# Modulation vectors of a two-block transformer: which MLP step computes which vector, and where VectorE's products and their sums over partitions are queued

## The chip, the cores and the metric

The kernel runs on one core of a Trainium2 chip. The metric is the device time of the whole program in microseconds (us). Five engines run side by side, each through its own queue of instructions in order: TensorE (PE; its weight loads are listed apart, as PEld), VectorE (DVE), ScalarE (ACT), GpSimd (POOL) and SyncE (SP), which issues the loads from memory. They wait for each other by semaphores.

## The reference, cut to what matters

A first block (a norm, two mixers, a mixture of experts) is followed by a second block of two layers, of which each is modulated by six vectors that come from one condition vector:

```python
cond = jax.nn.silu(c)                      # (1, 1024)
for i in range(2):
    mod = cond @ w_ada[i] + b_ada[i]       # 1024 x 6144
    sh1, sc1, g1, sh2, sc2, g2 = jnp.split(mod, 6, axis=-1)
    h = rms_norm_2(x, ln_mix_g[i]) * (1.0 + sc1[:, None, :]) + sh1[:, None, :]
    y = nsa_mixer(h, ...) if i == 0 else diff_mixer(h, ...)
    x = x + g1[:, None, :] * y
    h = rms_norm_2(x, ln_mlp_g[i]) * (1.0 + sc2[:, None, :]) + sh2[:, None, :]
    x = x + g2[:, None, :] * (jnp.square(jax.nn.relu(h @ w_mlp_in[i])) @ w_mlp_out[i])
```

There are 256 tokens of 1024 features, and the MLP is 4096 wide. The twelve vectors are numbered here as in the kernel, `mods[0]` to `mods[11]`, six to a layer: 5 is g2 of the first layer, 6 to 11 belong to the second. A vector is the condition times a weight of 1024 x 1024 in single precision, 4 MB.

## The kernel before

**Order of the work.** The kernel is written as one Python program, and a list scheduler (`schedule_with_timeline_sim=True`, line 2362) puts every engine's instructions into one fixed order, taking for each the place where its own simulation finds its operands ready. An instruction under `tc.issue_after(x)` is placed no earlier than x. Once placed, an engine goes through its queue in that order; where an instruction waits, all behind it wait.

**A vector on TensorE.** `ada_half` does half a vector: it loads two tiles of `w_ada` (1 MB each, tile `w`), and 32 matmuls add the condition's products into a bank `adaps`, four column strips side by side (in the order's listing 32 of the name `adaps<-w,cond`). VectorE copies or adds the bank to `ada_acc`. `ada_close` then sums over the four strips with two matmuls against `pick` (each shown as two in the trace; tile `adasum` of the pool `mm`), and VectorE adds the bias (`mod<-adasum,cols`).

**A vector on VectorE.** `ada_vector`, called four times for a vector, loads one tile of `w_ada` and adds two products of 128 x 1024 to the accumulator `adasum` in SBUF, one `TENSOR_SCALAR` for a vector's first and `SCALAR_TENSOR_TENSOR` for the other seven. With the fourth call, four matmuls against ones sum the accumulator over its partitions into `adaps` (`strips`, line 187; in the order's listing four of `adaps<-adasum,ones`), and ScalarE copies that to `ada_acc`; `ada_close` follows at the next call. There is one accumulator, so the next vector's first product waits for the strips of the one ahead.

**Where they are.** The first five halves come ahead of the first layer's attention. In it (`work(j)`, called for its 16 pairs) seven more are done, for j = 3 to 9, so that vector 5 is whole at its end. In the first layer's MLP (MLP 0), `mlp(0, ..., 11)` does vectors up to 10 on VectorE; vector 11 follows on TensorE after it, ahead of the second layer's attention. The second layer's MLP (MLP 1) does none.

**An MLP step.** The MLP goes in 8 steps of 512 hidden features, and the steps overlap: first the block `hp` (the product with `w_mlp_in`, line 448: 96 matmuls of 128 x 258 into four banks of `mm`), then the block `mlp` (the product of the step before with `w_mlp_out`, line 491: 96 matmuls of 128 x 256 into four banks of the pool `acc`). Each block takes two loaded tiles `w`, and each tile is split by halves into a high and a low part: ScalarE casts (`whi`, line 151), VectorE subtracts (`wlo`, line 152). There are three buffers of each, so that a cast waits until TensorE has used the pair three back. Behind an `hp` block VectorE and ScalarE form `hid` (`hb`, `relu`, squares). Three calls of `ada_vector` belong to a step, two after `hid`, one between the two tiles of `mlp`.

**Loads.** All 1 MB weight tiles come through one ring of 8 buffers by SyncE's queue. The tiles `adaps`, `adasum` and `hp` take turns in the four banks of `mm`.

Of the kernel before, what the change touches and what calls it, by code (L numbers as in the profile page):

```python
# [13 lines left out]
F32 = mybir.dt.float32  # L14
# [7 lines left out]
ALU = mybir.AluOpType  # L22
# [3 lines left out]
P = 128  # L26
T = 256
TX = T + 2
D = 1024
# [15 lines left out]
def block_kernel(ctx: ExitStack, tc: tile.TileContext, A: dict, out: bass.AP):  # L45

    nc = tc.nc
# [8 lines left out]
    def mm(shape=(P, 512), name="mm"):  # L56
        return mm_pool.tile(list(shape), F32, tag="mm", name=name)
# [117 lines left out]
    ada_at = [0, 0, 0.0]  # L175
# [42 lines left out]
    def ada_close():  # L218

        if not ada_open:  # L220
            return
        v = ada_open.pop()
        sp = mm(name="adasum")
        for c in range(2):
            nc.tensor.matmul(
                sp[:, 4 * c : 4 * c + 4], ada_acc[:, c * P : (c + 1) * P], pick, start=True, stop=True
            )
        nc.vector.tensor_tensor(
            mods[v].rearrange("p (j c) -> p c j", c=2),
            sp[:, 0:8].rearrange("p (c j) -> p c j", c=2),  # L230
            col("ada", v * KD, KD).rearrange("p (j c) -> p c j", c=2),
            op=ALU.add,
        )
# [8 lines left out]
            ada_at[2] -= 2.0  # L242
            ada_half()

    def ada_vector(acc):

        ada_close()
        v, q, _ = ada_at
        lay, i = divmod(v, 6)
        w = load(  # L250
            A["w_ada_2"][lay, 2 * q * P : 2 * (q + 1) * P, i * D : (i + 1) * D].rearrange("(k p) c -> p k c", p=P), D
        )
        for kk in range(2):
            c = cond[:, 2 * q + kk : 2 * q + kk + 1]
            if q + kk == 0:
                nc.vector.tensor_scalar(acc, w[:, kk, :], c, None, op0=ALU.mult)
            else:
                nc.vector.scalar_tensor_tensor(acc, w[:, kk, :], c, acc, op0=ALU.mult, op1=ALU.add)
        ada_at[1] = q + 1
        if q == 3:  # L260
            ps = mm(name="adaps")[:, :T]
            strips(ps, ones[:, 0:32], acc, True, True)
            nc.scalar.copy(ada_acc, ps)
            ada_at[:2] = [v + 1, 0]
            ada_open.append(v)

    def ada_until(v):
        while ada_at[0] < v:
            ada_half()
        if v - 1 in ada_open:  # L270
            ada_close()
# [168 lines left out]
    def proj_X_steps(w, c0, outs):  # L440

        for k0, t in colblock(w, c0, 512):
            for k1, hi, lo in halves(t):
                for kk in range(hi.shape[1]):
                    k = k0 + k1 + kk
                    for h in range(4):
                        for i, (a, b) in enumerate(passes((hi, lo), hX)):
                            nc.tensor.matmul(  # L448
                                outs[h],
                                a[:, kk, h * P : (h + 1) * P],  # L450
                                b[:, k, :],
                                start=(k == 0 and i == 0),
                                stop=(k == KD - 1 and i == 2),
                            )
                    yield
# [26 lines left out]
    def rows(w, r0, outs, acts, a0, first, after=None):  # L482


        t = load(w[r0 * P : (r0 + 2) * P, :].rearrange("(k p) c -> p k c", p=P), D)
        ada_credit(rate[0])
        parts = halves(t)

        def product(kk, hi, lo, dc):
            for i, (a, b) in enumerate(passes((hi, lo), acts)):  # L490
                nc.tensor.matmul(  # L491
                    outs[dc // 2][:, dc % 2, :],
                    a[:, 0, dc * P : (dc + 1) * P],
                    b[:, a0 + kk, :],
                    start=(first and kk == 0 and i == 0 and dc % 2 == 0),
                    stop=(after is not None and kk == 1 and i == 2 and dc % 2 == 1),
                )

        if after is None:
            for kk, hi, lo in parts:  # L500
                for dc in range(KD):
                    product(kk, hi, lo, dc)
            return
        with tc.manual_schedule(engines={mybir.EngineType.PE}):
            for pr in range(KD // 2):
                for kk, hi, lo in parts:
                    for dc in (2 * pr, 2 * pr + 1):
                        product(kk, hi, lo, dc)
                after(pr)
# [16 lines left out]
    def closing(banks, gate=None, st=None, each=None, feed=None):  # L526

        def after(pr):  # L530
            v = add_pair(pr, banks[pr], gate)
            last = pr == KD // 2 - 1
            if feed is not None:
                feed(pr)
                st.square(pr, v)
                if pr >= 2:
                    st.count(pr - 2)
                return
            if st is not None:
                if last and st.w is not None:  # L540
                    held["first"]["dve"] = added[0]
                st.square(pr, v)
            if st is not None:
                for p in range(pr - 2, pr + 1 if last else pr - 1):
                    if last and p == pr and st.w is None:
                        st.fill()
                    if p >= 0:
                        st.count(p)
            if each is not None:
                for p in range(pr - 1, pr + 1 if last else pr):  # L550
                    if p >= 0:
                        each(p)

        return after
# [1094 lines left out]
    def ct(name, shape, dt=F32, tag=None, **kw):  # L1649
        return pc.tile(list(shape), dt, name=name, tag=tag or name, **kw)  # L1650
# [87 lines left out]

    def mlp(lay, close, st, vectors):

        ada_sum = ct("adasum", (P, D), tag="klo")
        if ada_at[1]:
            ada_half()
        w_i, w_o = A["w_mlp_in_2"][lay], A["w_mlp_out_2"][lay]
        pend = None
        for j in range(9):
            rate[0] = 0.0
            if j < 8:
                hp = [(mm if j else acc)((P, TX), name="hp") for _ in range(4)]
                for n, _ in enumerate(proj_X_steps(w_i, j * 512, hp)):  # L1750
                    if j == 0 and n == 3:
                        st.count(2)
                        st.count(3)
                        rb = st.scale()
                both = n8("hid", F32R).rearrange("p (a k t) -> p a k t", a=2, k=4)
                for i in range(2):
                    r = sc((P, 2, T), name="relu")
                    b = pw.tile([P, 4], F32, tag="nm", name="hb")
                    for c in range(2):
                        nc.vector.tensor_copy(b[:, c : c + 1], hp[2 * i + c][:, T : T + 1])  # L1760
                        nc.vector.tensor_tensor(r[:, c, :], hp[2 * i + c][:, 0:T], rb, op=ALU.mult)
                        nc.scalar.activation(r[:, c, :], r[:, c, :], AF.Relu, bias=b[:, c : c + 1])
                    hi = both[:, 0, 2 * i : 2 * i + 2, :]
                    nc.scalar.activation(hi, r, AF.Square)
                    nc.scalar.activation(r, r, AF.Square)
                    nc.vector.tensor_tensor(both[:, 1, 2 * i : 2 * i + 2, :], r, hi.bitcast(F32), op=ALU.subtract)
                for _ in range(2):
                    if j and ada_at[0] < vectors:
                        ada_vector(ada_sum)
            if j == 0:  # L1770
                banks = [acc((P, 2, T), name="mlp") for _ in range(4)]
            if pend is not None:
                jj, bb = pend
                if jj == 7:
                    ada_close()
                    ada_until(6 * lay + 6)
                for c in (0, 2):
                    if c == 2 and ada_at[0] < vectors:
                        ada_vector(ada_sum)
                    after = close(banks) if jj == 7 and c == 2 else None  # L1780
                    rows(w_o, jj * 4 + c, banks, (bb[:, 0], bb[:, 1]), c, jj == 0 and c == 0, after)
            pend = (j, both)
# [395 lines left out]
    def work(j):  # L2178
        chains.tick(3)
        if 1 <= j < 5:  # L2180
            steps(second, 3)
        elif j >= 10:
            steps(first, 1)
        if 3 <= j < 10:
            ada_half()

    attention([(i, m) for i in range(8) for m in (1, 0)], pair_probs, pair_out, pair_tail, work)
# [16 lines left out]
    nc.vector.tensor_tensor(nlam, ls[:, 1:2], ls[:, 0:1], op=ALU.subtract)  # L2204
    nc.vector.tensor_scalar(nlam, nlam, -lam_init, None, op0=ALU.add)
    st = Stats()
    mlp(0, lambda banks: closing(banks, mods[5], st), st_x, 11)


    modulated(st, 1, 0, col("lnx", 8, 8))  # L2210
# [155 lines left out]
```

## Time and profile before

| | before |
|---|---|
| median of 3 runs | 1307.55 us |
| lowest and highest | 1306.39 and 1308.12 us |
| the profiled execution's own time | 1305.86 us |
| span of its trace | 1304.2 us |
| TensorE clock granted, mean | 0.99 of full |

The trace is of one execution. Its span leaves out 1.7 us around the program; its own time lies 1.7 us under the median of the runs. The stages that the change touches lie in the span's last 600 us: the first layer's attention from about 600 to 790 us, MLP 0 from 790 to about 985, the second layer's attention to 1113, MLP 1 to the end.

### The profile page before, as it was taken

The numbers are of one execution on the slowest core, as the hardware profiler recorded it, in microseconds if no ns is written. First come the engines' busy times: TensorE is split into PE (matmuls) and PEld (weight loads), VectorE is DVE, ScalarE is ACT, GpSimd is POOL, SyncE is SP. The second block draws the span as 40 slices with busy tenths as digits, with TensorE's granted clock in tenths as the row PEclk, the third lists the DMA queues.
The fourth block names the chain that finished last, engine by engine and source line by source line (L and its number), as shares of the span: only waits on it lengthen the run. The fifth ranks groups of instructions, "written<-read, shape, count | busy, mean of one in ns | idle before, by whom it ended". The sixth has DMA issues, their size and how long they took to land.

```text
span 1304.2 us, 22821 instructions
## 1 busy us (share of the span) xinstructions
PE 1260.6 (97%) x9471; PEld 998.6 (77%) x9471; DVE 651.8 (50%) x1268; ACT 511.8 (39%) x918; POOL 65.2 (5%) x92
## 2 busy tenths in 40 slices
PE   8999899999999999999998999999999999999998
PEld 7779565665555556556885679999997879999998
DVE  6765310130101111004776777698667787655554
ACT  7743211111101111113455656544544564654644
POOL 1010000000000000000410000000001120000000
PEclk9999899999999999998998999999999999999999
DMA  7997799999999999998554845599677532555510
GB/s 252 363 411 300 289 421 420 421 421 421 421 420 420 421 421 421 420 415 305 167 195 153 328 164 199 182 353 338 249 272 271 178 130 77 180 172 187 194 66 33
DMA packets 99157, 373.98 MB, mean 287 GB/s; under 512 B 10649, under 2 KB 14442, under 8 KB 74730
## 3 DMA queue, kind: packets, MB, share of 16 engines
q1 hardware_dynamic: 99050, 372.49, 75.1%
q8 instruction: 76, 1.25, 0.4%
q14 instruction: 31, 0.25, 0.1%
HBM read 371.41 MB, written 1.05 MB: 286 GB/s over the span
## 4 chain that ended last, share of the span: by engine, by line
PE 74%; issue 11%; DVE 2%; ACT 1%; POOL 0%; DVEq 0%; ACTq 0%; POOLq 0%
PE hp L448 14%; PE mlp L491 14%; PE gups L1429 13%; PE dps L1459 6%; PE dps L469 5%; PE sums L1477 3%; PE gps L1383 2%; PE oearly L584 2%; PE qp L469 2%; PE olate L491 2%; PE adaps L187 1%; PE kv L469 1%; PE opair L2119 1%; PE kcv L469 1%; PE ptps L2110 1%
## 5 line engine op out<-in xcount | busy, mean ns | idle before, releaser
L152 DVE TENSOR_TENSOR wlo<-w,whi 128x1024 fp32r<-128x1024 f32 (+1 forms) x222 | 269.7, 1218 | 160.9 <-ACT whi L151 158.6
L151 ACT CAST whi<-w 128x1024 fp32r<-128x1024 f32 (+1 forms) x222 | 230.5, 1043 | 251.0 <-PE hp L448 105.6
L1429 PE MATMUL gups<-w,xg 128*64 128x256 f32 x2048 | 236.2, 384 | 3.5 <-PEq L1287 3.5
L1429 PEld LDWEIGHTS gups<-w,xg 128*64 128x64 f32 x2048 | 145.6, 138 | 91.6 <-issue 22.6
L491 PE MATMUL mlp<-hid,whi 128*128 128x256 f32 x1024 | 184.0, 282 | 0.0
L491 PEld LDWEIGHTS mlp<-hid,whi 128*128 128x128 f32 x1024 | 157.2, 188 | 0.4 <-issue 0.4
L491 PE MATMUL mlp<-hid,wlo 128*128 128x256 f32 x512 | 144.8, 283 | 0.0
L448 PE MATMUL hp<-hT_lo,whi 128*128 128x258 f32 x512 | 144.0, 282 | 0.0
L448 PE MATMUL hp<-hT_hi,whi 128*128 128x258 f32 x512 | 143.7, 283 | 0.0
L448 PE MATMUL hp<-hT_hi,wlo 128*128 128x258 f32 x512 | 142.5, 282 | 0.0
L1441 DVE TENSOR_TENSOR h<-h,gups 128x256 f32<-128x256 f32 x32 | 13.5, 421 | 235.8 <-ACT h L1440 235.8
L1459 PE MATMUL dps<-w,hT 128*64 128x512 f32 x496 | 112.7, 596 | 5.1 <-ACT hT L1449 5.1
L491 PEld LDWEIGHTS mlp<-hid,wlo 128*128 128x128 f32 x512 | 96.4, 188 | 1.6 <-issue 1.6
L448 PEld LDWEIGHTS hp<-hT_lo,whi 128*128 128x128 f32 x512 | 96.7, 189 | 0.0
L448 PEld LDWEIGHTS hp<-hT_hi,whi 128*128 128x128 f32 x512 | 96.2, 188 | 0.0
L448 PEld LDWEIGHTS hp<-hT_hi,wlo 128*128 128x128 f32 x512 | 95.9, 189 | 0.0
L1440 ACT ACTIVATE h<-gups 128x256 f32<-128x256 f32 x32 | 12.3, 385 | 183.6 <-PE gups L1429 183.6
L1459 PEld LDWEIGHTS dps<-w,hT 128*64 128x64 f32 x496 | 34.1, 137 | 64.3 <-issue 53.0
L1470 DVE COPY ysb<-dps 64x512 f32<-64x512 f32 x31 | 21.2, 683 | 107.0 <-PE dps L1459 107.0
L1471 ACT COPY ysb<-dps 64x512 f32<-64x512 f32 x31 | 18.0, 582 | 139.0 <-DVE ysb L1470 139.0
L1477 PE MATMUL sums<-sw,ysb 128*128 128x256 f32 x256 | 61.3, 385 | 6.3 <-DVE ysb L1470 6.3
L1477 PEld LDWEIGHTS sums<-sw,ysb 128*128 128x128 f32 x256 | 46.4, 190 | 20.0 <-DVE ysb L1470 13.3
(539 smaller groups left out, 2014.5 us busy)
## 6 DMA issues: line engine op xcount, KB each, us to landing
w<-in_w_gate_dram SPq DMA_DIRECT2D x64, 1024.0 KB
w<-in_w_up_dram SPq DMA_DIRECT2D x64, 1024.0 KB
w<-in_w_down_dram SPq DMA_DIRECT2D x62, 1024.0 KB
w<-in_w_ada_dram SPq DMA_DIRECT2D x48, 1024.0 KB
w<-in_w_mlp_in_dram SPq DMA_DIRECT2D x32, 1024.0 KB
w<-in_w_mlp_out_dram SPq DMA_DIRECT2D x32, 1024.0 KB
w<-in_diff_w_in_dram SPq DMA_DIRECT2D x12, 1024.0 KB
w<-in_w_in_dram SPq DMA_DIRECT2D x10, 1024.0 KB
```

What stands on the lines that cost most here:

```text
L151: nc.scalar.copy(hi, v)
L152: nc.vector.tensor_tensor(lo, v, hi.bitcast(F32), op=ALU.subtract)
L448: nc.tensor.matmul(outs[h], a[:, kk, h * P : (h + 1) * P], b[:, k, :], start=(k == 0 and i == 0), stop=(k == KD - 1 and i == 2),)
L469: nc.tensor.matmul(outs[m], b[:, k, m * P : (m + 1) * P], a[:, kk, :], start=(k == 0 and i == 0), stop=(k == KD - 1 and i == 2),)
L491: nc.tensor.matmul(outs[dc // 2][:, dc % 2, :], a[:, 0, dc * P : (dc + 1) * P], b[:, a0 + kk, :], start=(first and kk == 0 and i == 0 and ...
L584: nc.tensor.matmul(banks[h // 2][:, h % 2, :], a[:, kk, h * P : (h + 1) * P], b[:, k, :], start=(k == 0 and i == 0 and h % 2 == 0), stop=( ...
L1383: nc.tensor.matmul(ps[:, j, :], part[:, m, k * P : (k + 1) * P], hot[:, m].rearrange("p e s -> p (e s)"), start=(n == 0), stop=(n == 3),)
L1429: nc.tensor.matmul(ps[j * 64 : (j + 1) * 64, s * 256 : (s + 1) * 256], xg[:, k, s0 : s0 + SLOTS], w[k // 4][:, k % 4, j * 256 : (j + 1) * ...
L1459: nc.tensor.matmul(dps[half * 64 : (half + 1) * 64, :], hT[:, c, j * 64 : (j + 1) * 64], dt[f // 2][:, f % 2, half * 512 : (half + 1) * 51 ...
L1470: nc.vector.tensor_copy(t[e2 * 64 : e2 * 64 + 64, 0:512], dps[0:64, :])
L1471: nc.scalar.copy(t[e2 * 64 : e2 * 64 + 64, 512:1024], dps[64:128, :])
L1477: nc.tensor.matmul(sums[k // 2][:, k % 2, :], t[:, k * P : (k + 1) * P], sw, start=(pr == 0 and k % 2 == 0), stop=(after is not None and k ...
```

## The change

Each vector is done one place later. In the attention of the first layer two halves fewer are done on TensorE (j = 3 to 7, up to vector 4); MLP 0 does vectors 5 to 9 on VectorE in place of 6 to 10; vector 10 takes the place of 11 on TensorE; vector 11 is done on VectorE in MLP 1, which had none. The products of a call are placed behind the last `hid` of their step (`low`). There are two accumulators, and a vector's strips are no longer issued with its last product but at a later place of the step (`ada_strips`), behind the last matmul of the block that was written ahead of that place (`last_product`).

```diff
-    def ada_vector(acc):
-        ada_close()
+    def ada_vector(acc, behind):
+        ada_strips()
         v, q, _ = ada_at
+        acc = acc[:, v % 2, :]
...
-            if q + kk == 0:
-                nc.vector.tensor_scalar(acc, w[:, kk, :], c, None, op0=ALU.mult)
-            else:
-                nc.vector.scalar_tensor_tensor(acc, w[:, kk, :], c, acc, op0=ALU.mult, op1=ALU.add)
+            with tc.issue_after(behind.ins):
+                if q + kk == 0:
+                    nc.vector.tensor_scalar(acc, w[:, kk, :], c, None, op0=ALU.mult)
+                else:
+                    nc.vector.scalar_tensor_tensor(acc, w[:, kk, :], c, acc, op0=ALU.mult, op1=ALU.add)
         ada_at[1] = q + 1
         if q == 3:
-            ps = mm(name="adaps")[:, :T]
-            strips(ps, ones[:, 0:32], acc, True, True)
-            nc.scalar.copy(ada_acc, ps)
-            ada_at[:2] = [v + 1, 0]
-            ada_open.append(v)
+            ada_at[:2] = [v + 1, 0]
+            ada_sums.append((v, acc))
+
+    def ada_strips():
+        ada_close()
+        if not ada_sums:
+            return
+        v, acc = ada_sums.pop(0)
+        ps = mm(name="adaps")[:, :T]
+        with tc.issue_after(last_product[0].ins):
+            strips(ps, ones[:, 0:32], acc, True, True)
+        nc.scalar.copy(ada_acc, ps)
+        ada_open.append(v)
...
-        ada_sum = ct("adasum", (P, D), tag="klo")
+        ada_sum = ct("adasum", (P, 2, D), tag="klo")
...
-                        ada_vector(ada_sum)
+                        ada_vector(ada_sum, low)
...
                 if jj == 7:
-                    ada_close()
                     ada_until(6 * lay + 6)
+                else:
+                    ada_strips()
...
-        if 3 <= j < 10:
+        if 3 <= j < 8:
             ada_half()
...
-    mlp(0, lambda banks: closing(banks, mods[5], st), st_x, 11)
+    mlp(0, lambda banks: closing(banks, mods[5], st), st_x, 10)
```

**What stands where on the engines.** In the listings a row is the line, the operation, what it writes and reads with the tile's number in the program, the shape, and how many such stand in a row.

TensorE in the first layer's attention, before, with the last of the seven halves and the one ahead of it (j = 8 and 9, the tiles `adaps_5949` and `adaps_6011`; `ptps` are transposes of the probabilities `p`, `opair` the products with the values):

```order
L225 MATMUL adasum_5945<-pick_99,adaacc_98 128x4 x2
L187 MATMUL adaps_5949<-w_5950,cond_85 32x256 x8
L187 MATMUL adaps_5949<-w_5960,cond_85 32x256 x8
L2119 MATMUL opair_5856<-pt_5943,vv_4688 64x128 x4
...
L2110 MATMUL ptps_6004<-ident_76,p_5925 128x128 x2
L187 MATMUL adaps_6011<-w_6012,cond_85 32x256 x8
L187 MATMUL adaps_6011<-w_6022,cond_85 32x256 x5
L2110 MATMUL ptps_6004<-ident_76,p_5925 128x128 x2
L187 MATMUL adaps_6011<-w_6022,cond_85 32x256 x3
```

These four rows of `adaps` are gone in the change, and so is the `adasum` of vector 5, which stands at the attention's end before; the last half there is that of j = 7, and matmuls of the first output half (`oearly`) stand earlier among the pairs.

TensorE in MLP 0 before, around the sum over partitions of vector 6 (`adaps_7210`), the first on VectorE:

```order
L491 MATMUL mlp_6791<-hid_6912,whi_7226 128x256 x2
L187 MATMUL adaps_7210<-adasum_6627,ones_83 32x256 x4
L491 MATMUL mlp_6791<-hid_6912,wlo_7227 128x256
L491 MATMUL mlp_6791<-hid_6912,whi_7226 128x256 x2
L491 MATMUL mlp_6791<-hid_6912,wlo_7227 128x256
L491 MATMUL mlp_6788<-hid_6912,whi_7230 128x256 x2
```

The same in the change, around the sum of vector 6 (`adaps_7447`, the second there):

```order
L509 MATMUL mlp_6743<-hid_7135,whi_7525 128x256 x2
L509 MATMUL mlp_6743<-hid_7135,wlo_7526 128x256
L187 MATMUL adaps_7447<-adasum_6579,ones_83 32x256 x4
L225 MATMUL adasum_7511<-pick_99,adaacc_98 128x4 x2
L466 MATMUL hp_7577<-hT_hi_74,whi_7583 128x258
L466 MATMUL hp_7577<-hT_lo_75,whi_7583 128x258
L466 MATMUL hp_7577<-hT_hi_74,wlo_7584 128x258
```

Before, the strips stood inside a block, and `adasum` well behind them; now both stand between the last matmul of a `mlp` block and the first of the next `hp`. Vectors 5 and 8 stand so too; those of 7 and 9 have their `adasum` well behind.

VectorE in the change, from the last `hid` but one of that step to the product that `adaps_7447` reads last (`w_7439`, `w_7443` are the last two tiles of vector 6, `w_7515` the first of vector 7):

```order
L1784 TENSOR_TENSOR hid_7416<-relu_7417,hid_7416 128x512
L152 TENSOR_TENSOR wlo_7584<-w_7581,whi_7583 128x1024
L1784 TENSOR_TENSOR hid_7416<-relu_7428,hid_7416 128x512
L261 SCALAR_TENSOR_TENSOR adasum_6579<-w_7439,cond_85,adasum_6579 128x1024
L259 TENSOR_SCALAR adasum_6579<-w_7515,cond_85 128x1024
L152 TENSOR_TENSOR wlo_7588<-w_7581,whi_7587 128x1024
L261 SCALAR_TENSOR_TENSOR adasum_6579<-w_7439,cond_85,adasum_6579 128x1024
L261 SCALAR_TENSOR_TENSOR adasum_6579<-w_7515,cond_85,adasum_6579 128x1024
L152 TENSOR_TENSOR wlo_7642<-w_7639,whi_7641 128x1024
L261 SCALAR_TENSOR_TENSOR adasum_6579<-w_7443,cond_85,adasum_6579 128x1024 x2
L228 TENSOR_TENSOR mod6_92<-adasum_7511,cols2_195 128x2x4
```

The two products of `w_7443` stand behind `wlo_7642` there, of a tile of the next `hp` block. ScalarE around the copy of that bank, in the change:

```order
L151 CAST whi_7583<-w_7581 128x1024
L1783 ACTIVATE relu_7428<-relu_7428 128x512
L151 CAST whi_7587<-w_7581 128x1024
L151 CAST whi_7641<-w_7639 128x1024
L280 COPY adaacc_98<-adaps_7447 128x256
L151 CAST whi_7645<-w_7639 128x1024
```

The copy stands directly behind the cast `whi_7641`. That cast takes the buffer of `whi_7525`, three back, which the last rows of the `mlp` block read. For vectors 5 and 8 the copy stands behind the like cast of their step too.

## Rows read from the trace of the kernel before

**Rows 1.** The page's chain of work that ended last, shares of the span.

```profile
PE 74%; issue 11%; DVE 2%; ACT 1%; POOL 0%; DVEq 0%; ACTq 0%; POOLq 0%
```

**Rows 2.** Windows by stage; columns as in the page, then clock, DMA share, GB/s.

```profile
790.00:990.00 200.00, 199.03 (x1711) 194.21 (x1714) 150.04 (x216) 104.48 (x148) 3.29 (x2) 1.00 0.76 265
1113.00:1304.00 191.00, 186.84 (x1568) 186.18 (x1567) 103.57 (x154) 97.29 (x134) 0.70 (x1) 1.00 0.42 139
```

**Rows 3.** Chain of waits in MLP 1: start, length, what, how many.

```profile
1137.70 11.40 PE mlp L491 x96
1149.10 11.46 PE hp L448 x96
```

**Rows 4.** Chain of waits in MLP 0, one step.

```profile
863.40 2.37 PE mlp L491 x20
865.77 0.57 PE adaps L187 x8
866.34 3.76 PE mlp L491 x30
870.10 0.34 PE adasum L225 x4
870.44 5.57 PE mlp L491 x46
876.01 11.47 PE hp L448 x96
```

**Rows 5.** Groups by line in MLP 0: count, busy us, mean ns, idle before.

```profile
L152 DVE TENSOR_TENSOR wlo<-w,whi 128x1024 fp32r<-128x1024 f32 x64 | 78.2, 1223 | 40.1 <-ACT whi L151 39.7
...
L151 ACT CAST whi<-w 128x1024 fp32r<-128x1024 f32 x65 | 68.1, 1049 | 86.6 <-PE hp L448 51.9 <-PE mlp L491 33.3 <-issue 1.3
...
L258 DVE SCALAR_TENSOR_TENSOR adasum<-w,cond,adasum 128x1024 f32<-128x1024 f32 x30 | 38.4, 1279 | 1.0 <-DMA w<-in_w_ada_dram 0.8
...
L1766 DVE TENSOR_TENSOR hid<-relu,hid 128x512 fp32r<-128x512 f32 x16 | 10.4, 684 | 0.0
...
L1765 ACT ACTIVATE relu<-relu 128x512 f32<-128x512 f32 x16 | 9.3, 624 | 0.0
...
L256 DVE TENSOR_SCALAR adasum<-w,cond 128x1024 f32<-128x1024 f32 x4 | 3.0, 752 | 2.4 <-PE adaps L187 2.4
```

**Rows 6.** Timeline in MLP 0 at a sum over partitions: start, length, instruction.

```profile
893.10 1.05 ACT L151 CAST whi<-w 128x1024 fp32r<-128x1024 f32 x1
...
893.10 0.64 PE L187 MATMUL adaps<-adasum,ones 128*32 128x256 f32 x8
...
894.05 0.37 ACT L263 COPY adaacc<-adaps 128x256 f32<-128x256 f32 x1
```

**Rows 7.** Chain of waits in the attention, at the half of j = 8.

```profile
733.38 1.93 PE adaps L187 x32
```

**Rows 8.** Waits of TensorE, 715 to 765 us: total, times, longest.

```profile
PE ptps L2110 <- DVE q L1827: 0.7, 1, 0.7
```

**Rows 9.** Waits of TensorE at the attention's end, 765 to 786 us.

```profile
PE olate L491 <- DVE oT L566: 0.9, 1, 0.9
...
PE opair L2119 <- ACT pt L2112: 0.7, 1, 0.7
```

**Rows 10.** Timeline of VectorE at the attention's end.

```profile
776.79 1.28 DVE L258 SCALAR_TENSOR_TENSOR adasum<-w,cond,adasum 128x1024 f32<-128x1024 f32 x1
777.98 0.16 DVE L228 TENSOR_TENSOR mod<-adasum,cols 128x8 f32<-128x8 f32 x1
```

**Rows 11.** Wait of TensorE, 680 to 700 us.

```profile
PE ptps L2110 <- DVE p L2103: 4.3, 1, 4.3
```

**Rows 12.** Windows of two us around that wait; the clock stands third from last.

```profile
690.00:692.00 2.00, 1.62 (x9) 1.66 (x9) 2.00 (x9) 0.99 (x5) 0.80 (x1) 0.50 0.00 0
692.00:694.00 2.00, 2.00 (x8) 1.15 (x7) 1.55 (x7) 0.59 (x3) 0.00 (x0) 0.50 0.01 4
694.00:696.00 2.00, 2.00 (x11) 1.15 (x12) 0.57 (x2) 1.38 (x5) 0.00 (x0) 0.74 0.00 0
```

## What the change will do to the time

> **What bounds the kernel now.** I read the page's chain of work that ended last first: TensorE holds 74% of it, and no other engine over 2% [rows 1]. So the question is what happens on TensorE, and the windows by stage say where it has room. In MLP 0 TensorE is busy for 199.0 of 200 us and VectorE for 150.0; in MLP 1 VectorE is busy for 103.6 of 191 us [rows 2]. The chain shows what a vector on VectorE costs TensorE today. A step of MLP 1, which has none, is 11.40 + 11.46 = 22.86 us without a gap [rows 3]. The step of MLP 0 that carries a vector is 2.37 + 0.57 + 3.76 + 0.34 + 5.57 + 11.47 = 24.08 us [rows 4]: the four matmuls of the strips and the two of `adasum`, with what they break, make 1.22 us, although they stand ready when TensorE comes to them. No wait stands in those rows. A wait there would be paid in full, since nothing else in the stage is as long as TensorE's own work.
>
> **What is removed: two halves in the attention.** The half of j = 8 takes 1.93 us of the chain [rows 7], that of j = 9 has as many matmuls; with the `adasum` of vector 5, at 0.34 us as in MLP 0 [rows 4], that is 4.20 us. It isn't all won. Around j = 8 TensorE waits for VectorE's chain of `q`, `p` and the masks, with 0.7 us the longest wait in 50 us [rows 8]; a half put there partly fills time in which VectorE was late anyway. I take 0.8 us off and count 3.4 us. All of the j = 8 half hidden would leave 2.3 us.
>
> **What is moved: the products out of the attention's end.** Six products of vector 6, one of 0.75 and five of 1.28 us [rows 5], stand among the attention's last softmax steps today; the last of them begins at 776.79 us [rows 10], directly ahead of TensorE's waits for `pt` (0.7 us) and for `oT` (0.9 us) [rows 9]. In the change the products are pinned behind a `hid` of the MLP, the last transposes come earlier in TensorE's order, and other output matmuls can cover both waits: 1.6 us, with 0 as the bound if the last transposes wait for something else. The attention together: -5.0 us, between -2.3 and -5.8.
>
> **What is added in MLP 0: waits at the strips.** Five vectors are summed there as before, so the 1.22 us each stay. What changes is the place: for vectors 5, 6 and 8 strips and `adasum` stand back to back between a `mlp` block and the next `hp`.
>
> First, `adasum` needs ScalarE's copy of the bank. In the change the copy stands behind a cast that is released by the very end of the `mlp` block. One row has the like of it: cast and strips both begin at 893.10 us, the cast takes 1.05, the copy begins at 894.05 and ends 1.32 us after the strips began [rows 6], while TensorE is through with them after 0.57 [rows 4]. That leaves 0.75 us and a hand-over of some 0.05: 0.8 us for vector 5 and as much for vector 8.
>
> Second, vector 6. Its strips wait for the last product of `w_7443`. On VectorE this stands behind `wlo_7642`; that needs the cast `whi_7641`, whose buffer is free only when TensorE has used `whi_7525`, at the end of the `mlp` block that stands directly ahead of the strips. So the strips can't be ready when TensorE reaches them, whatever VectorE did before. Counted from the end of that block: the cast ends at 1.0 us, then `wlo` 1.22 and two products of 1.28 [rows 5], 4.8 us, or 4.6 since the rows of VectorE overlap by 0.08 each. That is the lower bound. VectorE's queue makes it later. The cast `whi_7583` is free to begin when the first half of the block, 48 matmuls ahead of its end, is done, at -5.7 us; 1.05 later a square of 0.62, then at -4.0 VectorE's row: `hid` 0.68, a product 1.28, a first product 0.75, `wlo` 1.22, two products, `wlo` 1.22, two products: 10.27 us of the groups' means [rows 5], less 8 overlaps of 0.08: 9.6. The end is at 5.6 us; 6.2 without the overlaps is the upper bound. I take 5.6. Behind the strips on TensorE stand `adasum` and the whole next `hp` block, whose weights are long split: nothing of it can pass. After the wait the copy is in nobody's way, but `adasum` needs it at once: 0.37 us [rows 6] and two hand-overs, 0.45 us. Vectors 5 and 8 read their last product one tile earlier; by the same count from the same rows it ends 0.4 us ahead of the block's end, so no wait, with up to 1 us as the bound. Vectors 7 and 9 have their products and the copy done well before. Vector 6 therefore costs 6.05 us and the three together 7.65 us, between 6.2 and 10.
>
> **The clock.** An idle TensorE of this length has an example in the trace: it waits 4.3 us for `p` [rows 11] and afterwards runs at half the granted clock (0.50, the 1.2 GHz level) for 1.62 + 2.00 us and about 1.04 of the next two (0.74 on average), 4.66 us of work [rows 12]. Half of that is lost: 2.3 us. I take the same for the wait of vector 6, and nothing as the bound. The Trainium skill, "TensorE: Matmul & The Clock Gate", section "Part 1: The HAM clock gate (the "warmup" mystery)", says that the throttled clock is the default and activity lifts it; by it the sum has these 2.3 us, without it 2.3 less, and the example in the trace agrees with the page.
>
> **What is added in MLP 1.** Vector 11 was 32 matmuls twice on TensorE after MLP 0, and vector 10 takes that place, so nothing changes there but a `mod` of 0.16 us [rows 10] or two that come later in the second layer's attention: 0.2 us. In MLP 1 four loads, eight products and one sum are new. VectorE has 87 us of room in 191 and the loads take the DMA from 139 GB/s nowhere near the 265 of MLP 0 [rows 2], so only the sum costs: 1.2 us, as in MLP 0, with 2 as the bound, if the copy stands behind a cast.
>
> **The sum.** -5.0 + 7.65 + 2.3 + 0.2 + 1.2 = +6.35 us. Against the profiled execution's own 1305.86 us that is 1312.2; the median of the runs shown lies 1.7 us higher, so I expect a median of 1307.55 + 6.35 = 1313.9 us. 2.6 us (0.2%) is about what the measurement can tell from no change.
>
> **The rivals.**
> - *The strips of vector 6 don't wait.* This is the case on the other side. It decides at the end of the `mlp` block: if the product ends ahead of it, 6.05 and 2.3 us go, and the sum is -2.0: 1305.5 us. For it speaks that VectorE has a quarter of MLP 0 free and that the order was made for no wait; against it the chain of buffers above, which holds whatever the speed. Were the two copies early too, it would be 1303.9.
> - *The clock stays up.* The wait is there, and the gate doesn't fall: +4.05, 1311.6 us. The example has a wait 1.3 us shorter with a fall.
> - *The attention gives little.* The two halves come out of time that VectorE sets, and the end keeps its waits: VectorE gets three `wlo` earlier there, as the loads come sooner. With -2.3 the sum is +9.05: 1316.6 us. Against it: TensorE has one wait of 0.7 us around j = 8 and none of note up to the attention's end.
> - *More waits than vector 6.* If 5 and 8 wait for their products by the 1 us of the bound: +8.35, 1315.9 us.
>
> **How the numbers follow.** My forecast has a chance of 0.42; no wait 0.22, of which half with a gain over 2.6 us; the clock stays up 0.13; little from the attention 0.13; more waits 0.10. Slower by over 0.2% is everything with the wait, less a little for the attention's gain being larger than its bound: 0.75; within 0.2% 0.13; faster 0.12. The range leaves out the upper tail of the last two together (+11) and the early copies: 1305 to 1318 us; the likeliest case's own range is 1311 to 1316.
>
> **What would show it.** In the profile after: a wait of TensorE at line 187 for VectorE's product of 5 to 6 us, once, in the second vector of MLP 0, with a granted clock of 0.50 behind it; waits of 0.8 us at line 225 for the copy, twice; MLP 0 longer by some 10 us; the last matmul of the first attention about 5 us earlier; a step of MLP 1 with 1.2 us more. I am wrong if the strips of vector 6 find their products done, which would mean that the cast ahead of them was not held by the end of the block, or if the attention gives clearly more than 5.8 us.

## The result, and the profile after

The changed kernel took 1312.97 us in the median of 5 runs (1312.87 to 1314.1), the kernel before, run beside it, 1306.39 (1302.75 to 1308.12): the ratio is 1.0058, with a 95% interval of 1.0044 to 1.0072, 7.6 us slower (differences here and below are the ratio less one, times the median of before; the two medians themselves lie 6.6 us apart). One run of the fifth experiment below took 3191.98 us, and its ratio is that of the other eleven. The profiled execution took 1313.35 us; its span is 1311.7 us, 7.5 more than that of before.

I cut the span at four places that every kernel here has, the first starts of a tile's matmuls as the view of that tile gives them (`scores` and then the first `mlp` for the first layer's attention and MLP 0's first `hp`; `dps` for the second layer; the first `hp` of MLP 1; the end). The table is used for all kernels below, with one profiled execution for each. In its first column the changed kernel stands 0.8 us above its two variants with the same order on TensorE there (strips a step later, two products left out). That is the clock: behind the wait near the start of this attention it reads 0.50 in the changed kernel's windows of two us from 688 to 694 us, in the two variants only from 690 to 692, and 0.7 of the 0.8 us have come about by 695 us. In the changed kernel the four columns are 8.3 us longer than before, and what lies ahead of the first `scores` was 0.8 us shorter: the 7.5 of the spans.

| kernel | first attention, to the first `mlp` | MLP 0, to `dps` | second attention | MLP 1 and the end |
|---|---|---|---|---|
| before | 132.8 | 174.1 | 118.7 | 195.1 |
| changed | 128.7 | 185.3 | 118.7 | 196.3 |
| place only | 130.1 | 174.2 | 124.8 | 196.5 |
| pins and late strips only | 130.8 | 185.6 | 117.8 | 195.0 |
| changed, strips a step later | 127.9 | 174.8 | 118.7 | 196.3 |
| changed, two products left out | 127.9 | 178.3 | 118.7 | 196.3 |
| place only, vector 11 pinned | 130.2 | 174.1 | 118.7 | 196.3 |
| pins, strips a step later, old place | 131.7 | 174.1 | 118.9 | 195.1 |
| changed, without pins | 130.5 | 175.9 | 125.0 | 196.9 |

So the change took 4.1 us off the attention, put 11.2 on MLP 0 and 1.2 on MLP 1. The windows by stage of the changed kernel, as in [rows 2]:

```profile
790.00:990.00 200.00, 191.75 (x1606) 188.18 (x1608) 147.97 (x204) 98.72 (x139) 0.69 (x1) 0.98 0.77 273
1113.00:1304.00 191.00, 191.00 (x1611) 190.45 (x1610) 116.67 (x174) 101.55 (x142) 0.69 (x1) 1.00 0.47 160
```

In MLP 0 TensorE is now busy for 191.8 of 200 us and its clock reads 0.98; the 1113-to-1304 window of MLP 1 has VectorE busy for 116.7 us in place of 103.6. The waits of TensorE in MLP 0 (total, times, longest), neither of which is there before:

```profile
PE adaps L187 <- DVE adasum L261: 6.3, 1, 6.3
PE adasum L225 <- ACT adaacc L280: 1.9, 3, 0.7
```

One wait of 6.3 us at the strips, three of together 1.9 us at `adasum`. The timeline of ScalarE and VectorE ahead of the long one (start, length, instruction, and in brackets what ended an idle time):

```profile
866.02 1.23 DVE L152 TENSOR_TENSOR wlo<-w,whi 128x1024 fp32r<-128x1024 f32 x1 [0.21 <-ACT whi L151]
...
867.17 0.69 DVE L1784 TENSOR_TENSOR hid<-relu,hid 128x512 fp32r<-128x512 f32 x1
...
867.77 1.28 DVE L261 SCALAR_TENSOR_TENSOR adasum<-w,cond,adasum 128x1024 f32<-128x1024 f32 x1
...
868.97 0.75 DVE L259 TENSOR_SCALAR adasum<-w,cond 128x1024 f32<-128x1024 f32 x1
...
869.63 1.22 DVE L152 TENSOR_TENSOR wlo<-w,whi 128x1024 fp32r<-128x1024 f32 x1
...
870.63 1.04 ACT L151 CAST whi<-w 128x1024 fp32r<-128x1024 f32 x1 [1.80 <-PE mlp L509]
870.76 2.47 DVE L261 SCALAR_TENSOR_TENSOR adasum<-w,cond,adasum 128x1024 f32<-128x1024 f32 x2
...
873.15 1.22 DVE L152 TENSOR_TENSOR wlo<-w,whi 128x1024 fp32r<-128x1024 f32 x1
...
874.29 2.60 DVE L261 SCALAR_TENSOR_TENSOR adasum<-w,cond,adasum 128x1024 f32<-128x1024 f32 x2
```

The last matmul of the `mlp` block ends at 870.7 us; the cast begins at 870.63, set free by a `mlp` matmul after 1.80 us of idle time. VectorE never pauses from `hid` at 867.17 on, and the last product ends at 876.89. The `wlo` that needs that cast begins at 873.15, long after the cast ended at 871.67: VectorE's queue, not the cast, set the end. What follows on TensorE, from the chain of waits, and the clock in windows of two us (PE busy, clock, DMA share, GB/s):

```profile
877.04 1.11 PE adaps L187 x8
...
878.17 0.38 ACT adaacc L280
...
878.60 1.02 PE adasum L225 x4
879.62 12.88 PE hp L466 x96
892.50 11.40 PE mlp L509 x96
```

```profile
870.00:872.00 2.00, 0.71 (x7) 1.00 0.15 18
872.00:874.00 2.00, 0.00 (x0) 1.00 0.83 262
874.00:876.00 2.00, 0.00 (x0) 0.89 1.00 383
876.00:878.00 2.00, 0.96 (x8) 0.50 0.99 392
...
880.00:882.00 2.00, 2.00 (x12) 0.50 1.05 407
882.00:884.00 2.00, 2.00 (x17) 0.91 0.71 268
```

TensorE idles from 870.7 to 877.0 us. The granted clock still reads 1.00 in 872 to 874, falls in 874 to 876 and comes back in 882 to 884. The `hp` block in between takes 12.88 us where the block before the change takes 11.47 [rows 4]. The end of MLP 0 shows a second fall of the clock, which before does not have. First two pieces of the chain and a window of before, then the same of the changed kernel:

```profile
987.93 0.71 PE rbps L358 x4
988.64 1.86 PE adaps L187 x32
988.00:990.00 2.00, 2.00 (x32) 1.00 1.02 392
```

```profile
993.54 1.23 PE rbps L376 x4
994.76 2.00 PE adaps L187 x32
992.00:994.00 2.00, 1.91 (x18) 0.50 0.81 266
```

Here `rbps` spreads the factor of the next norm over the partitions and follows 1.6 us of GpSimd (`rs_r`) in both kernels; the `adaps` behind it belong to the vector that is done on TensorE. The two pieces are 0.66 us longer in the changed kernel.

One of the two copies of vectors 5 and 8, as [rows 6]:

```profile
845.74 1.05 ACT L151 CAST whi<-w 128x1024 fp32r<-128x1024 f32 x1 [1.79 <-PE mlp L509]
...
845.75 0.64 PE L187 MATMUL adaps<-adasum,ones 128*32 128x256 f32 x8
...
846.69 0.36 ACT L280 COPY adaacc<-adaps 128x256 f32<-128x256 f32 x1
...
847.11 0.61 PE L225 MATMUL adasum<-pick,adaacc 128*128 128x4 f32 x4 [0.72 <-ACT adaacc L280]
```

The strips begin with the cast, the copy waits for its end, and `adasum` begins 1.36 us after the strips. In MLP 1 the strips of vector 11 stand in the chain at 0.57 us between two blocks, with no wait:

```profile
1166.82 11.39 PE mlp L509 x96
1178.22 0.57 PE adaps L187 x8
1178.79 11.22 PE hp L466 x92
```

At the attention's end, of the four waits from before that had 2.7 us, two are left; those for `pt` and `oT` [rows 9] are gone:

```profile
PE olate L509 <- DVE wlo L152: 0.8, 1, 0.8
PE olate L509 <- ACT whi L151: 0.3, 1, 0.3
```

### The profile page after: what moved, and what is told of

It is laid out like the page before. It is cut to its first block, busy times and chain, and to the rows that moved or that the text cites. A ratio compares the mean times of both kernels' runs of the same rounds, so it can differ in the third digit from the quotient of the medians.

```text
span 1311.7 us, 22702 instructions
## 1 busy us (share of the span) xinstructions
PE 1260.0 (96%) x9415; PEld 1000.0 (76%) x9415; DVE 659.7 (50%) x1274; ACT 511.4 (39%) x919; POOL 64.1 (5%) x92
## 3 DMA queue, kind: packets, MB, share of 16 engines
q8 instruction: 76, 1.25, 0.4%
## 4 chain that ended last, share of the span: by engine, by line
PE 72%; issue 12%; DVE 3%; ACT 2%; DMA 0%; POOL 0%; DVEq 0%; POOLq 0%; ACTq 0%
PE hp L466 14%; PE mlp L509 13%; PE gups L1447 12%; PE dps L1477 6%; PE dps L487 5%; PE sums L1495 3%; PE gps L1401 2%; PE oearly L602 2%; PE qp L487 2%; PE olate L509 2%; PE kv L487 1%; PE kcv L487 1%; PE opair L2138 1%; PE adaps L187 1%; PE ptps L2129 1%
```

## The experiments

**Only the place.** The kernel before with two lines changed:

```diff
-        if 3 <= j < 10:
+        if 3 <= j < 8:
...
-    mlp(0, lambda banks: closing(banks, mods[5], st), st_x, 11)
+    mlp(0, lambda banks: closing(banks, mods[5], st), st_x, 10)
```

> Only the place is changed: two halves fewer in the attention, vectors 5 to 9 in MLP 0, vector 11 in MLP 1; one accumulator, no pins and the strips with the last product, as before the change. First theory (what costs time is where the strips stand, and the place itself pays): the halves give about 3.4 us, the sum in MLP 1 costs 1.2, a late mod 0.2, MLP 0 has no wait at line 187 or 225 and stays as long as before, and the products of vector 5 stay in the attention's end with its 1.6 us of waits: about 2 us faster than the kernel before, some 9 us faster than the changed kernel. Rival (the place costs: one vector more on VectorE in the MLPs slows them): within 2 us of the changed kernel, 5 to 7 us slower than before, with MLP 0 or MLP 1 longer without a wait at the strips.

Measured: 1310.57 us against 1304.2, ratio 1.0044 (1.0029 to 1.006), 5.7 us slower. The time is the rival's, but the place of the loss is neither's: MLP 0 is as long as before (174.2), MLP 1 is 1.4 us longer, the first attention gained 2.7, and the second layer's attention, of which I had thought nothing, is 6.1 us longer. Waits of TensorE there:

```profile
PE ptps L1732 <- DVE dsm L2248: 4.9, 1, 4.9
PE olate L491 <- DVE res L521: 1.3, 1, 1.3
PE tps L2297 <- ACT p L1726: 0.8, 1, 0.8
```

The wait at `ptps` was 2.8 us before. With two more of 0.6 and 0.3 us, the new waits are 5.1 of the 6.1 us; with the rest goes a longer fall of the clock, which reads 0.50 from 1074 to 1078 us here and from 1078 to 1080 before. The chain of waits leads through VectorE's products of vector 11, which without pins stand among the softmax steps of that attention, and through their loads (two rows of the chain, then VectorE's timeline with its idle time in brackets):

```profile
1063.36 5.40 DMA w<-in_w_ada_dram
...
1071.94 5.22 DMA w<-in_w_ada_dram
```

```profile
1068.78 0.75 DVE L256 TENSOR_SCALAR adasum<-w,cond 128x1024 f32<-128x1024 f32 x1 [1.04 <-DMA w<-in_w_ada_dram]
...
1077.19 1.28 DVE L258 SCALAR_TENSOR_TENSOR adasum<-w,cond,adasum 128x1024 f32<-128x1024 f32 x1 [2.17 <-DMA w<-in_w_ada_dram]
...
1094.77 1.29 DVE L258 SCALAR_TENSOR_TENSOR adasum<-w,cond,adasum 128x1024 f32<-128x1024 f32 x1 [1.83 <-DMA w<-in_w_ada_dram]
```

A product whose tile isn't there yet holds up all of VectorE's queue, and the softmax of the last heads behind it. VectorE stands idle for 1.04, 2.17 and 1.83 us of these loads, not for their whole 5 us.

**Only the pins, the accumulators and the late strips.** The changed kernel with those two lines as they were before.

> Only the pins, the two accumulators and the late strips; seven halves in the attention, vectors 6 to 10 in MLP 0, none in MLP 1, as before. First theory: the second vector of MLP 0 (now vector 7) waits about 6.3 us at its strips, three copies are waited for with 0.6 us each, the clock falls once for 2.3 us, and the attention's end loses 1.6 us of waits since the products are out of it: about 9 us slower than the kernel before, MLP 0 about 11 us longer. Rival (the place costs): as fast as before within 2 us, or faster by the 1.6 us.

Measured: 1314.01 us against 1304.2, ratio 1.0069 (1.0054 to 1.0084), 9.0 us slower, as expected. MLP 0 is 11.5 us longer, and its waits are those of the changed kernel to the tenth (6.3 us once, 1.9 us in three), now at vector 7. The second attention, 0.9 us shorter than before, has the same order on TensorE and the same wait of 2.8 us; here the clock stays at 1.00 behind that wait, where before it falls.

**The strips a step later.**

```diff
-            ada_sums.append((v, acc))
+            ada_sums.append((v, acc, step[0]))
...
-        if not ada_sums:
+        if not ada_sums or ada_sums[0][2] == step[0]:
             return
-        v, acc = ada_sums.pop(0)
+        v, acc, _ = ada_sums.pop(0)
...
     def ada_until(v):
+        step[0] = -1
...
             rate[0] = 0.0
+            step[0] = j
```

> The changed kernel, but a vector's strips are not issued in the step of its last product: they wait for the first place of the next step. First theory: the products are long done there and the strips stand inside a mlp block with adasum well behind them, so the wait of 6.3 us, the copies' 1.9 us and the fall of the clock go (about 10 us); what the attention gave stays: about 10 us faster than the changed kernel, 3 us faster than the kernel before. Rival (VectorE is late by itself, and strips anywhere in the step wait for it): the wait moves into the block, and the time stays within 3 us of the changed kernel.

Measured: 1301.69 us against 1304.2, ratio 0.9981 (0.9971 to 0.9991), 2.5 us faster than before and, by the two ratios, some 10 faster than the changed kernel. MLP 0 is 0.7 us longer than before and has no wait at the strips; the 0.7 us are the fall of the clock at its end, where `rbps` takes 1.22 us and the `adaps` behind it 2.02, against 0.71 and 1.86. A step with a vector reads in the chain as in [rows 4], piece by piece:

```profile
855.17 2.37 PE mlp L512 x20
857.54 0.57 PE adaps L187 x8
858.11 3.76 PE mlp L512 x30
861.87 0.34 PE adasum L225 x4
862.21 5.57 PE mlp L512 x46
```

**Two products left out.** The changed kernel without the last two of the eight products of vector 6, so that its sum lacks them:

```diff
             c = cond[:, 2 * q + kk : 2 * q + kk + 1]
+            if (v, q) == (6, 3):
+                continue
             with tc.issue_after(behind.ins):
```

> The changed kernel without the last two of the eight products of vector 6 (of the tile w_7443, which is loaded all the same), so that its strips wait for the second product of w_7439; all instructions of TensorE stand in the same order. By the trace of the changed kernel that product ends about 1.3 us behind the mlp block, so the wait falls from 6.3 to about 1.3 us. If the fall of the clock behind the wait costs time of its own (first theory), the kernel gains 5.0 and about 2.3 us, some 7 us, and no window behind the strips shows a clock under 1.00. If TensorE loses nothing by the clock there (rival), it gains 5.0 us.

(TensorE's order is that of the changed kernel but for one `hp` matmul behind the strips of vector 6 and six `dps` matmuls of the second attention.)

Measured: 1304.69 us against 1304.2, ratio 1.0002 (0.9992 to 1.0012). MLP 0 is 7.0 us shorter than in the changed kernel. The wait at the strips fell from 6.3 to 1.5 us, 4.8 us; the clock reads 1.00 behind it, and the pieces behind it in the chain, with two windows of the clock, are

```profile
870.35 0.67 PE adaps L187 x8
...
871.47 0.61 PE adasum L225 x4
872.08 11.59 PE hp L468 x96
883.68 11.40 PE mlp L511 x96
```

```profile
870.00:872.00 2.00, 1.17 (x13) 1.00 0.87 246
872.00:874.00 2.00, 2.00 (x18) 1.00 1.01 405
```

The changed kernel has 1.11, 1.02 and 12.88 us there: strips 0.44, `adasum` 0.41, `hp` 1.29 longer, together 2.14 us that went with the clock. 4.8 + 2.1 = 6.9, the 7.0 of the table. So the theory's 7 us held, and not the rival's 5.0.

**The place, with vector 11 pinned.** The first experiment, with the products of vector 11 placed behind the last `hid` of their step:

```diff
+            with ExitStack() as es:
+                if v == 11:
+                    es.enter_context(tc.issue_after(behind.ins))
```

> The first experiment (only the place) with one addition: the products of vector 11 alone are pinned behind the last hid of their step. In the first experiment the second layer's attention and MLP 1 together were 7.5 us longer than before, with six of the eight products of vector 11 among the attention's last steps. If those products on VectorE's queue made it (theory), that part is 1 to 3 us longer than before here (the sum's 1.2 and perhaps a copy), the attention of the first layer stays 2.7 us shorter, MLP 0 as before: 0 to 2 us faster than the kernel before. Rival (the four loads more in the ring make it): still 5 us or more longer, and 3 us or more slower than before.

Measured: 1303.63 us against 1305.16, ratio 0.9991 (0.9979 to 1.0004): the theory's range, and no difference from before that stands clear of the interval. The second attention is back at 118.7 us and MLP 1 at 196.3. The loads are as many; with the products behind `hid`, a late load no longer holds up the softmax.

**The old place, with pins and strips a step later.** The third experiment with the seven halves and vectors 6 to 10 of before.

> The third experiment (pins, two accumulators, strips in the step after) with the vectors in their old places: seven halves in the attention, vectors 6 to 10 in MLP 0, none in MLP 1. It asks what the place alone is worth once no strips wait. By the second and third experiments' stages: the attention 2.1 us shorter than before, MLP 0 0.8 longer, the rest up to 1.0 shorter: 1.5 to 2.3 us faster than before, so that the place is worth less than 1 us. Rival (the place pays what the forecast said, 3.4 us of halves less 1.4 us): 2 us slower than the third experiment, 0.5 us faster than before.

Measured: 1303.76 us against 1305.16, ratio 0.9995 (0.9985 to 1.0005). The rival was nearer: against the third experiment the place is worth 0.14%, 1.8 us, though the two intervals overlap. In the table it is 3.8 us in the first attention, less 1.2 in MLP 1 and 0.7 in MLP 0; of these, some 0.8 in the attention are a longer fall of the clock here, and the 0.7 a fall at the end of MLP 0 that only the third experiment has.

**Without pins.** The changed kernel without `issue_after(behind.ins)` around the products.

> The changed kernel without the pins: the products may be queued as early as their loads allow; two accumulators and the late place of the strips stay. If the waits of MLP 0 come from the late strips alone (rival), MLP 0 stays about 10 us longer than before. If it takes both, products held behind hid and strips that follow in the same step (theory), the strips stand inside the mlp blocks with no wait at line 187 or 225, MLP 0 is as long as before within 1 us, and the second layer pays some 7 us for unpinned products of vector 11 as in the first experiment: 4 to 5 us slower than before.

Measured: 1312.41 us against 1305.16, ratio 1.0055 (1.0041 to 1.007); 7.2 us slower, more than the 4 to 5 expected. The theory held in its places, not in the sum: the second attention is 6.3 us longer, as in the first experiment, the first attention gained 2.3, MLP 1 lost 1.8, and MLP 0 1.8 where I had said 1. The one wait of TensorE there is at the very end of the stage, of 1.0 us as in the kernel before, and none is at a strip:

```profile
PE rbps L376 <- POOL rs_r L304: 1.0, 1, 1.0
```

The four stages together are 7.6 us longer; the 1.0 us by which the stages ahead of `scores` were shorter in this profile leaves the 6.6 of the spans. Of MLP 0's 1.8 us, 1.6 lie in the two pieces at its end, where the clock reads 0.50 from 986 to 988 us: `rbps` takes 1.14 us against the 0.71 of before, and the `adaps` behind it 3.05 against 1.86:

```profile
985.88 3.05 PE adaps L187 x32
```

## Why the prediction was right

The forecast was +6.35 us and a median of 1313.9; the runs gave +7.6 us by the ratio and a median of 1312.97, beside runs of before that lay 1.2 us lower than those I had. That the two medians lie within 1 us is in part luck: the lower runs of before make up for a rise that was 1.25 us larger than the forecast. By its steps:

- *The attention, -5.0 us.* 4.1 in this profile; the 4.9 of the two kernels with the same order there have a shorter fall of the clock in them. By halves: the place alone gives 2.6 to 2.7 (first, fifth experiment), below my 3.4 but above the 2.3 of the bound; the pins alone give 1.1 (sixth; the 2.0 of the second has 0.9 of the clock), below my 1.6, and 0.3 us of the wait for `oT` is left there. Both halves were taken too high.
- *The copies, 0.8, 0.8 and 0.45 us.* 1.9 us in three waits against 2.05.
- *The wait of vector 6, 5.6 us.* 6.3 us. The mechanism and the row of instructions were as written; its length on VectorE, 9.7 us from `hid` on, is the 9.6 of the sum. The term was too small because `hid` began 3.5 us ahead of the block's end and not 4.0: a `wlo` from 866.02 to 867.25 us stood ahead of it, as in the order that I had listed, and I had not counted it. Another 0.15 us passed from the last product to the strips. I also gave the cast at the end of the block as the reason why the strips can't be ready; the measured end was set by VectorE's queue, and no run tests the lower bound of 4.6 us that the cast would set. (The lower end of the three vectors together, 6.2 us, leaves out vector 6's own copy; with it, it is 6.65.)
- *The clock, 2.3 us.* 2.14 us, by the fourth experiment. That it would fall at all was not sure: behind the wait of 2.8 us in the second attention it fell before and stayed up in the second experiment.
- *MLP 1 and the second attention, 1.4 us.* 1.2 and 0.0.
- *Not in the sum:* 0.9 us of MLP 0 (11.2 less 6.3, 1.9 and 2.1). 0.66 us of it is the second fall of the clock, at the end of MLP 0. The third, fourth and seventh experiments have that fall too, with 0.7, 0.8 and 1.8 us left over, and the second has it with 1.2; before and the first, fifth and sixth have none, and their MLP 0 takes 174.1 or 174.2 us. What decides whether the clock falls there is open.

What the prediction missed lies outside the sum. It gave the pins only a gain of 1.6 us in one attention. The first and fifth experiments show that with the vectors in their new place a pin on vector 11 keeps 6 us out of the second attention. And it had no alternative for the strips: neither pins nor late strips made the waits by themselves (the seventh experiment has the late strips and no wait, the third has the pins and none). The wait of 6.3 us came where products held behind `hid` met a sum asked for in the same step, and there only at the second vector of MLP 0.

## What to carry to other kernels

Moving work to an engine with room costs what waits for its result, so look for the first reader in the order: an instruction that stands between two full blocks of the bounding engine, and waits for one that has just been queued, stops that engine for the whole queue ahead of it. Hold early work back (the pins) and give its reader a step more: the pins with the reader in the same step lost 7.6 us, the new place without pins 5.7 and 7.2; pins only on the vector that needs them lost nothing. A later reader without pins was not run. And where a scheduler fills gaps with work that waits for a load, the whole in-order queue waits for that load.

## What the runs showed of the hardware

The granted clock fell during an idle time of 6.3 us, read 0.50 (1.2 GHz) in the windows from 876 to 882 us, and 2.14 us of TensorE's time went with it; behind a wait of 1.5 us at the same place it stayed at 1.00. It fell late in the wait: in the window from 872 to 874 us, which has no matmul at all, it still read 1.00.

The length of a wait does not decide it alone. The wait of 2.8 us at `ptps` in the second attention, with the same order on TensorE, was followed by 0.83, 0.50 and 0.82 in the windows from 1076 to 1082 us before, and by 1.00 in each window from 1082 to 1090 us in the second experiment, whose second attention is 0.9 us shorter. And at the end of MLP 0 the clock left 1.00 in a window in which TensorE was busy throughout (990 to 992 us of the changed kernel, 2.00 of 2.00 us, clock 0.90). Falls of these kinds made differences of 0.7 to 1.6 us between stages, so one profile of each kernel does not settle a difference of that size until the clock's rows have been looked at.
